# A gated MLP's down projection as seven products of quarter blocks, with weight sums made by DMAs in DRAM

## The chip, the cores and the metric

The kernel runs on one core of a Trainium2 chip. The metric is the device time of one execution in microseconds (us); lower is better. "The profile" is one execution recorded by the hardware profiler; its times count from the first instruction of that execution.

## What is computed

One layer of an encoder trunk on 512 tokens of width 1024: a token mixing stage (attention heads beside a gated recurrent group), a cross-attention into 256 memory tokens, and a gated MLP. The last stage is the one that matters here; the rest is named only so that the stages of the profile can be told apart.

```python
def conv_ffn(h, w_up, conv_w, conv_b, w_down):
    u = h @ w_up                       # 512 x 1024  @  1024 x 5632
    ...                                # depthwise convolution over 3 positions
    gate, val = jnp.split(acc, 2, axis=-1)
    return (jax.nn.silu(gate) * val) @ w_down     # 512 x 2816  @  2816 x 1024

x = x + rmsnorm(conv_ffn(h, ...), post_ffn_g)
```

## The kernel before

**Precision.** Every product is made from numbers split into a high part and a low part of the type fp32r. `mm3` (L149) issues three matmuls for one product: high by high (L150), high by low (L151), low by high (L152). A split (`split`, L103) is a ScalarE cast of the source (L104) and a subtraction on VectorE (L105).

**Weights.** All weights lie in DRAM as units of 128 x 1024 floats, in the order in which they are used. `load_w` (L115) issues the load of the next unit on SP's queue (L117) into one of two "raw" buffers; `issue` (L121) casts and subtracts it into one of four "wh" and four "wl" buffers. For the units 7 to 41 the low part is made another way: a negated copy of the high part (L129 on ScalarE or L131 on POOL), to which a DMA from POOL's queue adds the weights (L132). `unit` (L143) hands out the next unit, and `issue_ahead` keeps three units ahead of it.

**Big buffers.** Activations live in 16 buffers of 8 KB per partition, all called "big" (L94). A tile takes one when it is first written and gives it back after its last use. PSUM has eight banks: two each of the names b, s, c and o.

**The MLP.** For each of 22 chunks of 128 channels, `proj_fm` (L252) makes a gate and a value block from one unit each (24 matmuls), and `conv` (L899) evacuates it: ScalarE scales and adds the bias (L902), VectorE adds the two neighbours (L903, L905), ScalarE applies silu to the gate (L908), VectorE multiplies value and gate (L913) into the tiles `acts`, four chunks to a tile.

**Down projection (L932 to L966).** Eight PSUM banks hold the whole result, four row blocks of 128 tokens by two column halves. For each of the 22 chunks the activations of 512 tokens are split, a unit of weights (128 x 1024) is taken, and 8 x 3 matmuls are issued. The last four chunks are gone through row block by row block, so that the norm and the residual of one block (`residual_part`, L206: square on ScalarE L209, a small chain on POOL L178 and L181, gain on VectorE L211; `residual_add`, L214, L216) and its store (L966) run while TensorE works on the next.

**Order.** The source is written in the order of the data flow, with a `weave` of generators in the earlier stages. The order on each engine is made when the program is built, from which instruction is ready; `tc.issue_after(...)` holds an instruction behind another one on its engine (used around L403 to L425 for the first loads). Each engine then runs its own list strictly in order. POOL's list holds the row scales of all norms (L168, L169, L178, L181), the DMAs of the gains (L163) and the accumulating DMAs (L132). Near the start, L168 makes the row scales of x, from which TensorE spreads the row factors (L405) that the first evacuated projections are multiplied with.

Of the kernel before, what the change touches and what calls it, by code (L numbers as in the profile page):

```python
# [18 lines left out]
P = 128  # L19
# [55 lines left out]
def layer(tc, io, out):  # L75
# [8 lines left out]
    b8 = pool("b8", bufs=16)  # L84
    t4 = pool("t4", bufs=2)
    t2 = pool("t2", bufs=4)

    def small():
# [23 lines left out]
    pending, last_pow, last_mm = deque(), [None], [None]  # L112
    issued, taken, last_load = [0], [0], [None]

    def load_w():  # L115
        raw = rawp.tile([P, 1024], F32, name="raw", tag="raw")
        last_load[0] = nc.sync.dma_start(raw, io["w"][issued[0]]).ins  # L117
        issued[0] += 1
        return raw

    def issue():  # L121
        i = issued[0]
        raw = load_w()
        wh = wp.tile([P, 1024], F32R, name="wh", tag="wh")
        wl = wp.tile([P, 1024], F32R, name="wl", tag="wl")
        if i in NEG_SCALAR or i in NEG_POOL:
            nc.scalar.copy(wh, raw)  # L127
            if i in NEG_SCALAR:
                nc.scalar.mul(wl, wh.bitcast(F32), -1.0)  # L129
            else:  # L130
                nc.gpsimd.tensor_scalar(wl, wh.bitcast(F32), -1.0, 0.0, op0=ALU.mult, op1=ALU.add)  # L131
            nc.gpsimd.dma_start(wl, io["w"][i], accum_op=ALU.add)  # L132
        else:
            split(wh, wl, raw)
        pending.append((wh, wl))
# [13 lines left out]
    def mm3(o, a, b, start, stop):  # L149
        nc.tensor.matmul(o, a[0], b[0], start=start, stop=False)  # L150
        nc.tensor.matmul(o, a[0], b[1], start=False, stop=False)  # L151
        last_mm[0] = nc.tensor.matmul(o, a[1], b[0], start=False, stop=stop).ins  # L152

    def blk(b):
        return slice(b * P, (b + 1) * P)
# [16 lines left out]
    def half(c):  # L172
        return slice(c * 512, c * 512 + 512)
# [137 lines left out]
    def drain(g):  # L311
        for _ in g:
            pass
# [580 lines left out]
    hT = new_act()  # L894
    turns = res_second(ox, range(4), kv["x0"], between(x, g_post, g_pre, hT))

    acts, gates = [], {}

    def conv(c, i, u):  # L899
        g = c * NF + i  # L900
        a = tmp2()
        nc.scalar.activation(a, u, ACT.Identity, scale=cw[:, g, 1:2], bias=cw[:, g, 3:4])  # L902
        nc.vector.scalar_tensor_tensor(out=a[:, 1:], in0=u[:, :T - 1], scalar=cw[:, g, 0:1], in1=a[:, 1:],  # L903
                                       op0=ALU.mult, op1=ALU.add)
        nc.vector.scalar_tensor_tensor(out=a[:, :T - 1], in0=u[:, 1:], scalar=cw[:, g, 2:3], in1=a[:, :T - 1],  # L905
                                       op0=ALU.mult, op1=ALU.add)
        if c == 0:
            nc.scalar.activation(a, a, ACT.Silu)  # L908
            gates[i] = a
        else:  # L910
            if i % 4 == 0:
                acts.append(big([P, 4, T]))
            nc.vector.tensor_mul(acts[-1][:, i % 4, :], gates.pop(i), a)  # L913

    up_tags = "bsco"
    first = [(c, i) for i in range(2) for c in range(2)]
# [16 lines left out]
    y = [[bank(y_tags[c][b]) for c in range(2)] for b in range(NB)]  # L933
    parts = {}

    def down(b, c, kc, w):
        hi, lo = parts[kc // 4]
        mm3(y[b][c], (hi[:, kc % 4, blk(b)], lo[:, kc % 4, blk(b)]), (w[0][:, 0, half(c)], w[1][:, 0, half(c)]),
            kc == 0, kc == NF - 1)

    last = NF - 4
    ws = {}
    for kc in range(NF):
        if kc % 4 == 0:
            parts[kc // 4] = (big([P, 4, T], F32R), big([P, 4, T], F32R))
        split(parts[kc // 4][0][:, kc % 4, :], parts[kc // 4][1][:, kc % 4, :], acts[kc // 4][:, kc % 4, :])
        w = unit(1)
        if kc >= last:
            ws[kc] = w
            continue  # L950
        for b in range(NB):
            for c in range(2):
                down(b, c, kc, w)
    for b in range(NB):
        ss, done = small(), []
        for c in range(2):
            for kc in range(last, NF):
                down(b, c, kc, ws[kc])
            done.append(residual_part(ss, y[b][c], g_post, c, half(c), c == 1, "ta" if c else "th"))
        if b == NB - 1:  # L960
            yg, cols = done.pop()
            for q in range(2):
                done.append((yg[:, q * 256:q * 256 + 256], slice(cols.start + q * 256, cols.start + q * 256 + 256)))
        for i, part in enumerate(done):
            residual_add(ss, part, x[b])
            (nc.sync, nc.scalar)[i % 2].dma_start(out[blk(b), part[1]], x[b][:, part[1]])  # L966
    assert taken[0] == N_UNITS
    ctx.close()


def pack_weights(w_in, w_xkv, w_out, w_xq, w_xo, w_up, w_down):
# [24 lines left out]
    for c in range(8):  # L996
        fm(w_xkv, c * P)
    tm(w_xkv, 1024)
    tm(w_out, 0, MIX_ORDER)
    tm(w_out, 512, MIX_ORDER)  # L1000
    tm(w_xkv, 1536)
    for c in range(8):
        fm(w_xq, c * P)
    tm(w_xo, 0)
    tm(w_xo, 512)
    for i in range(NF):
        fm(w_up, i * P)
        fm(w_up, FF + i * P)
    for kc in range(NF):
        units.append(w_down[kc * P:(kc + 1) * P])  # L1010
    assert len(units) == N_UNITS
    return np.stack(units)


def shape_constants():
# [42 lines left out]
```

## Time and profile before

| | us |
|---|---|
| time, median of 3 runs (839.5 to 841.27) | 839.54 |
| the profiled execution, its own time | 839.84 |
| span of that execution, first to last instruction | 838.1 |
| TensorE busy | 826.9 |
| VectorE busy | 488.0 |
| ScalarE busy | 430.8 |
| POOL busy | 91.8 |

PE is TensorE's matmul side, PEld its weight loads, DVE VectorE, ACT ScalarE, POOL GpSimd, SP the engine that only issues DMAs; a q behind a name is its sequencer. "L105" is line 105 of the kernel. A group's row reads: line, engine, operation, output<-inputs by the program's names, shapes, count | busy us, mean ns of one | idle time of the engine just before, and what ended it. A row of the timeline reads: start, duration, engine, line, operation, and in brackets the idle time before it and its releaser. A row of the stages reads: stretch, its length, then busy time (and instructions) of PE, PEld, DVE, ACT and POOL, then the granted TensorE clock, the busy share of the 16 DMA engines, and GB/s. The digits of the DMA row on the page are tenths in 40 equal slices of the span. A queue's row reads: packets, MB, share of 16 engines' span.

### The profile page before, as it was taken

Reading aid. Unit: us, or ns where it says so; the run is one execution under the profiler, and the core shown is the slowest. Engines: PE = TensorE matmul, PEld = TensorE weight load, DVE = VectorE, ACT = ScalarE, POOL = GpSimd, SP = SyncE. Lnnn points to the kernel's source line nnn. Section 1 sums busy time; section 2 is a strip of 40 time slices with the busy share of each in tenths; the row PEclk is TensorE's granted clock in tenths of the full one; section 3 lists DMA queues with packets and bytes.
Section 4 is the critical chain, followed back from the end, with each engine's and each line's share of the span. In section 5 each row is a group of like instructions: output and inputs, shape, how many; then the busy total and the mean of one; then the engine's idle time right before and its main releaser. Section 6 shows DMA issues by size and latency. Waiting matters only on the chain.

```text
span 838.1 us, 11074 instructions
## 1 busy us (share of the span) xinstructions
PE 826.9 (99%) x4304; PEld 700.8 (84%) x4304; DVE 488.0 (58%) x759; ACT 430.8 (51%) x743; POOL 91.8 (11%) x148
## 2 busy tenths in 40 slices
PE   9999999999999999999999999999999999999996
PEld 7888888889898888888888998888888888888885
DVE  5347577389886866854535765555555557722224
ACT  6676656379888864644534553333333335522221
POOL 0111201145123102200001300000000000000001
PEclk9999999999999999999999999999999999999999
DMA  8696654558677551342311332222222233222212
GB/s 317 191 280 142 158 114 99 129 127 192 139 169 156 127 186 40 126 151 76 101 50 51 122 107 99 101 101 100 99 84 94 101 101 101 100 91 90 97 50 101
DMA packets 29860, 101.81 MB, mean 121 GB/s; under 512 B 3952, under 2 KB 4464, under 8 KB 29808
## 3 DMA queue, kind: packets, MB, share of 16 engines
q1 hardware_dynamic: 22752, 77.38, 26.9%
q0 software_dynamic: 5760, 20.97, 13.9%
q10 hardware_dynamic: 1296, 2.76, 0.9%
q8 instruction: 34, 0.56, 0.3%
q14 instruction: 18, 0.15, 0.1%
HBM read 99.00 MB, written 2.10 MB: 121 GB/s over the span
## 4 chain that ended last, share of the span: by engine, by line
PE 95%; DVE 2%; DMA 1%; ACT 1%; issue 0%; SPq 0%; POOL 0%; POOLq 0%; DVEq 0%
PE ps_b L150 10%; PE ps_b L152 10%; PE ps_b L151 10%; PE ps_s L152 6%; PE ps_s L151 6%; PE ps_s L150 6%; PE ps_o L150 6%; PE ps_o L152 6%; PE ps_o L151 6%; PE ps_c L150 4%; PE ps_c L152 4%; PE ps_c L151 4%; PE ps_c L517 3%; PE ps_o L762 2%; PE ps_s L740 2%; PE ps_o L750 2%
## 5 line engine op out<-in xcount | busy, mean ns | idle before, releaser
L105 DVE TENSOR_TENSOR wl<-raw,wh 128x1024 fp32r<-128x1024 f32 x93 | 113.8, 1224 | 199.6 <-ACT wh L104 199.4
L104 ACT CAST wh<-raw 128x1024 fp32r<-128x1024 f32 x93 | 98.0, 1053 | 205.2 <-PE ps_o L152 71.4
L150 PE MATMUL ps_b<-big,wh 128*128 128x512 f32 (+1 forms) x320 | 118.2, 370 | 0.8 <-DVE big L105 0.8
L152 PE MATMUL ps_b<-big,wl 128*128 128x512 f32 (+1 forms) x320 | 116.6, 364 | 0.0
L151 PE MATMUL ps_b<-big,wh 128*128 128x512 f32 (+1 forms) x320 | 116.5, 364 | 0.0
L150 PEld LDWEIGHTS ps_b<-big,wh 128*128 128x128 f32 x320 | 60.3, 189 | 9.7 <-DVE big L105 0.9
L152 PEld LDWEIGHTS ps_b<-big,wl 128*128 128x128 f32 x320 | 60.3, 189 | 9.3
L151 PEld LDWEIGHTS ps_b<-big,wh 128*128 128x128 f32 x320 | 60.4, 189 | 9.1
L178 POOL TENSOR_SCALAR small<-small 128x1 f32<-128x1 f32 x40 | 13.9, 348 | 439.2 <-ACT tmp L209 420.2
L543 DVE TENSOR_TENSOR big<-big 128x512 f32<-128x512 f32 x64 | 48.4, 761 | 15.1 <-PE ps_c L517 8.8
L150 PE MATMUL ps_s<-wh,big 128*128 128x512 f32 (+1 forms) x140 | 53.7, 383 | 0.4 <-DVE big L105 0.4
L152 PE MATMUL ps_s<-wh,big 128*128 128x512 f32 (+1 forms) x140 | 53.1, 379 | 0.0
L151 PE MATMUL ps_s<-wl,big 128*128 128x512 f32 (+1 forms) x140 | 53.0, 379 | 0.0
L127 ACT CAST wh<-raw 128x1024 fp32r<-128x1024 f32 x35 | 36.8, 1050 | 23.7 <-PE ps_b L151 13.1
L150 PE MATMUL ps_o<-wh,big 128*128 128x512 f32 (+1 forms) x124 | 47.9, 386 | 0.0
L151 PE MATMUL ps_o<-wl,big 128*128 128x512 f32 (+1 forms) x124 | 46.8, 377 | 0.0
L152 PE MATMUL ps_o<-wh,big 128*128 128x512 f32 (+1 forms) x124 | 46.7, 377 | 0.0
L105 DVE TENSOR_TENSOR big<-ps_o,big 128x512 fp32r<-128x512 f32 x54 | 37.1, 688 | 13.4 <-ACT big L104 13.2
L132 POOL DMA_DIRECT2D wl<-in_w_dram x35 | 30.8, 881 | 119.5 <-ACT wl L129 104.5
L104 ACT CAST big<-ps_o 128x512 fp32r<-128x512 f32 x54 | 31.7, 586 | 19.4 <-PE ps_o L865 7.5
L150 PE MATMUL ps_b<-wh,big 128*128 128x512 f32 x92 | 36.9, 401 | 0.0
L151 PE MATMUL ps_b<-wl,big 128*128 128x512 f32 x92 | 36.0, 392 | 0.0
(245 smaller groups left out, 1935.7 us busy)
## 6 DMA issues: line engine op xcount, KB each, us to landing
raw<-in_w_dram SPq DMA_DIRECT2D x131, 512.0 KB, 3.2
wl<-in_w_dram POOLq DMA_DIRECT2D x35, 512.0 KB, 5.5
big<-in_x_dram SPq DMA_DIRECT2D x8, 512.0 KB, 6.4
big<-in_xt_dram SPq DMA_DIRECT2D x3, 512.0 KB, 8.2
big<-in_mem_dram ACTq DMA_DIRECT2D x2, 512.0 KB, 11.9
out_dram<-big SPq DMA_DIRECT2D x4, 256.0 KB, 2.0
out_dram<-big ACTq DMA_DIRECT2D x3, 256.0 KB, 2.0
big<-in_xt_dram SPq DMA_DIRECT2D x2, 256.0 KB, 3.4
```

The costliest lines, as they stand in the source:

```text
L104: nc.scalar.copy(hi, src)
L105: (eng or nc.vector).tensor_sub(lo, src, hi.bitcast(F32))
L127: nc.scalar.copy(wh, raw)
L132: nc.gpsimd.dma_start(wl, io["w"][i], accum_op=ALU.add)
L150: nc.tensor.matmul(o, a[0], b[0], start=start, stop=False)
L151: nc.tensor.matmul(o, a[0], b[1], start=False, stop=False)
L152: last_mm[0] = nc.tensor.matmul(o, a[1], b[0], start=False, stop=stop).ins
L517: nc.tensor.matmul(o[:, b, :], kc[:, blk(b)], pat(qk, b * P, [[2 * m, P // (2 * m)], [T + m, 2], [1, m]]), start=True, stop=True)
L543: nc.vector.tensor_tensor(out=c, in0=c, in1=pat(tt, toff + off, [[2, npair], [gap, 2], [0, m]]), op=ALU.mult)
L740: nc.tensor.matmul(s, qT[h // 4][:, h % 4, blk(qb)], kT[:, 2 * (h // 4) + c, :], start=c == 0, stop=c == 1)
L750: nc.tensor.transpose(o[:, c, :], e[:, 0, blk(c)], ident)
L762: nc.tensor.matmul(o, vv[:, c, h // 4].rearrange("p a d -> p (a d)"), pt[:, j, c, :], start=c + j == 0, stop=c == 3 and j == 1)
```

## The change

The down projection is cut into quarters. The 512 tokens are halved (0 to 255, 256 to 511), the 22 chunks are split into 11 even and 11 odd ones, the 1024 columns are halved. With A for the activations (second index: even or odd chunks) and W for the weights, the four quarters of the result need eight products of quarters if computed directly; the change makes seven (the Winograd form of Strassen's scheme), each of 256 tokens by 11 chunks by 512 columns, and combines them by additions.

- **Weights.** `pack_down` stores the four quarters w11, w12, w21, w22 as 128 x 5632 each. Four sums are needed as well: t1 = w11 + w12, t3 = w22 + w12, t2 = t1 + w22, t4 = t2 + w21 (the signs are put in the combinations). `new_sums(u)` makes slice u of the four: for each a tile in DRAM, a DMA from POOL's queue that copies one operand into it, and a second one that adds the other. Six slices make 48 DMAs; the call stands in the up projection's loop after the chunks 2, 5, 8, 11, 14 and 17. Slices are 1024 columns wide, the last 512.
- **Units.** The 22 units of the down projection become 42: seven products by six slices. Units 0 to 109 are as before. A unit of a product is loaded from the quarter or from the sum in DRAM.
- **Activations.** `conv` writes even and odd chunks to separate tiles; after each eight chunks (and at the end) `group_sides` makes three differences on VectorE: S = A21 - A22, A11 - S, and A21 - A11 in place of A21. The left sides of the seven products are split group by group (three groups of 4, 4 and 3 chunk pairs), three groups ahead; in the group of index 1, products 1 to 6, the low part is made by a negated copy on POOL and an accumulating DMA.
- **Products.** Each product uses two PSUM banks (row blocks 0 and 1 of its half). What is combined is copied or added on ScalarE and VectorE when a product ends. Rows 256 to 511 are finished after the sixth product, rows 0 to 255 after the seventh, whose last four chunk pairs are gone through block by block.

```diff
-N_UNITS = 132
+N_WHOLE, N_UNITS = 110, 152
+NP = NF // 2
+GROUPS = ((0, 4), (4, 8), (8, NP))
+PRODUCTS = (("w11", "b"), ("t2", "s"), ("t1", "c"), ("w22", "o"), ("t3", "s"), ("t4", "c"), ("w21", "b"))
+SUMS = (("t1", "w11", "w12"), ("t3", "w22", "w12"), ("t2", "t1", "w22"), ("t4", "t2", "w21"))
+LAY_AHEAD = 3
+NEG_GROUP = frozenset((p, 1) for p in range(1, 7))
...
+            p, u = divmod(i - N_WHOLE, 6)
+            cols = width(u)
+            raw = raw[:, :cols.stop - cols.start]
+            nc.sync.dma_start(raw, weight_block(PRODUCTS[p][0], cols))
...
+    def new_sums(u):
+        n = width(u).stop - width(u).start
+        for out_name, first_name, second_name in SUMS:
+            t = dram.tile([P, n], F32, name="sum_%s_%d" % (out_name, u), tag="sum_%s_%d" % (out_name, u))
+            nc.gpsimd.dma_start(t, weight_block(first_name, width(u)))
+            nc.gpsimd.dma_start(t, weight_block(second_name, width(u)), accum_op=ALU.add)
+            sums.setdefault(out_name, []).append(t)
+
+    def group_sides(g):
+        n = GROUPS[g][1] - GROUPS[g][0]
+        even, odd = acts[g]
+        t = big([P, 2, 4, 256])
+        sides.append(t)
+        nc.vector.tensor_sub(t[:, 0, :n], even[:, :n, half_t[1]], odd[:, :n, half_t[1]])
+        nc.vector.tensor_sub(t[:, 1, :n], even[:, :n, half_t[0]], t[:, 0, :n])
+        nc.vector.tensor_sub(even[:, :n, half_t[1]], even[:, :n, half_t[1]], even[:, :n, half_t[0]])
...
+            if i % 8 == 7 or i == NF - 1:
+                group_sides(i // 8)
...
+        if i % 3 == 2 and i // 3 < 6:
+            new_sums(i // 3)
...
+    def left_side(p, g):
...
+        if p == 3:
+            nc.vector.tensor_sub(sides[g][:, 1, :n], odd[:, :n, half_t[0]], sides[g][:, 1, :n])
+        src = (even[:, :n, half_t[0]], sides[g][:, 1, :n], sides[g][:, 0, :n], sides[g][:, 1, :n],
+               even[:, :n, half_t[1]], odd[:, :n, half_t[1]], odd[:, :n, half_t[0]])[p]
+        t = big([P, 2, 4, 256], F32R)
+        hi, lo = t[:, 0, :n], t[:, 1, :n]
+        if (p, g) in NEG_GROUP:
+            nc.scalar.copy(hi, src)
+            nc.gpsimd.tensor_scalar(lo, hi.bitcast(F32), -1.0, 0.0, op0=ALU.mult, op1=ALU.add)
+            nc.gpsimd.dma_start(lo, src, accum_op=ALU.add)
+        else:
+            split(hi, lo, src)
...
+    for p, (_, tag) in enumerate(PRODUCTS):
+        y = [bank(tag) for _ in range(2)]
+        for j in range(NP if p < 6 else last):
+            if j % 4 == 0:
+                lay_ahead(3 * p + j // 4)
+            if j % 2 == 0:
+                w = take()
+            for b in range(2):
+                products(y, p, j, w, b)
+        if p == 0:
+            y1, u = tmp4([P, 2, 512]), tmp4([P, 2, 512])
+            for b in range(2):
+                nc.scalar.copy(y1[:, b], y[b])
+        elif p == 1:
+            for b in range(2):
+                nc.vector.tensor_sub(u[:, b], y[b], y1[:, b])
...
+        for i, cols in enumerate(pieces):
+            nc.vector.tensor_add(c11[:, cols], y[b][:, cols], y1[:, b, cols])
+            parts[b].append(residual_part(rows[b], c11[:, cols], g_post, 1 + i, cols, i == b, "th"))
+        finish(b, rows[b], parts[b])
```

More of the change, by code (lines that the diff above doesn't have):

```diff
@@ L113, in layer, with weight_block, width @@
     issued, taken, last_load = [0], [0], [None]
+    sums = {}
+    def weight_block(name, cols):
+        if name in sums:
+            return sums[name][cols.start // 1024][:, :cols.stop - cols.start]
+        return io["wd"][("w11", "w12", "w21", "w22").index(name)][:, cols]
+    def width(u):
+        return slice(u * 1024, min(u * 1024 + 1024, NP * 512))
     def load_w():
         raw = rawp.tile([P, 1024], F32, name="raw", tag="raw")
-        last_load[0] = nc.sync.dma_start(raw, io["w"][issued[0]]).ins
+        i = issued[0]
+        if i < N_WHOLE:
+            last_load[0] = nc.sync.dma_start(raw, io["w"][i]).ins
+        else:
[3 more added lines that the diff above has]
+            nc.sync.dma_start(raw, weight_block(PRODUCTS[p][0], cols))
         issued[0] += 1
@@ L910, in conv @@
         else:
[L911 to L913 removed]
+            if i % 8 == 0:
+                acts.append([big([P, 4, T]) for _ in range(2)])
+            nc.vector.tensor_mul(acts[-1][i % 2][:, i // 2 % 4, :], gates.pop(i), a)
+            if i % 8 == 7 or i == NF - 1:
+                group_sides(i // 8)
     up_tags = "bsco"
@@ L942, in layer @@
[L942 to L963, printed above, removed]
+    def left_side(p, g):
+        n = GROUPS[g][1] - GROUPS[g][0]
+        even, odd = acts[g]
+        if p == 3:
[8 more added lines that the diff above has]
+            nc.gpsimd.dma_start(lo, src, accum_op=ALU.add)
+        else:
+            split(hi, lo, src)
+        return hi, lo
@@ new lines, in layer, with lay_ahead, products, take @@
+    order = [(p, g) for p in range(7) for g in range(3)]
+    laid = {}
+    def lay_ahead(i):
+        while len(laid) < min(len(order), i + LAY_AHEAD):
+            laid[order[len(laid)]] = left_side(*order[len(laid)])
+    def products(y, p, j, w, b):
+        hi, lo = laid[p, j // 4]
+        ac, wc = (slice(None), j % 4, blk(b)), half(j % 2)
+        mm3(y[b], (hi[ac], lo[ac]), (w[0][:, wc], w[1][:, wc]), j == 0, j == NP - 1)
+    def take():
+        taken[0] += 1
+        issue_ahead()
+        return pending.popleft()
@@ new lines, in layer @@
+    lay_ahead(20)
+    ws = {}
+    for j in range(last, NP):
+        ws[j] = take() if j % 2 == 0 else ws.get(j - 1, w)
+    for b in range(2):
+        c11 = tmp2(tag="tq")
+        pieces = [slice(0, 256), slice(256, 512)] if b else [slice(0, 512)]
+        for j in range(last, NP):
+            products(y, 6, j, ws[j], b)
+        for i, cols in enumerate(pieces):
+            nc.vector.tensor_add(c11[:, cols], y[b][:, cols], y1[:, b, cols])
+            parts[b].append(residual_part(rows[b], c11[:, cols], g_post, 1 + i, cols, i == b, "th"))
+        finish(b, rows[b], parts[b])
@@ L1008, in pack_weights, with pack_down @@
         fm(w_up, FF + i * P)
-    for kc in range(NF):
-        units.append(w_down[kc * P:(kc + 1) * P])
-    assert len(units) == N_UNITS
+    assert len(units) == N_WHOLE
     return np.stack(units)
+def pack_down(w_down):
+    w = w_down.reshape(NP, 2, P, 2, 512).transpose(1, 3, 2, 0, 4)
+    return w.reshape(4, P, NP * 512)
 def shape_constants():
```

41 lines of the change are left out of this document (31 added, 10 removed).

## The prediction

> **What bounds the kernel now.** I read the page from the top: engines, slices, DMA queues, chain, then the DMA issues.
>
> ```profile
> PE 826.9 (99%) x4304; PEld 700.8 (84%) x4304; DVE 488.0 (58%) x759; ACT 430.8 (51%) x743; POOL 91.8 (11%) x148
> ...
> DMA  8696654558677551342311332222222233222212
> ...
> q1 hardware_dynamic: 22752, 77.38, 26.9%
> q0 software_dynamic: 5760, 20.97, 13.9%
> ...
> PE 95%; DVE 2%; DMA 1%; ACT 1%; issue 0%; SPq 0%; POOL 0%; POOLq 0%; DVEq 0%
> ...
> raw<-in_w_dram SPq DMA_DIRECT2D x131, 512.0 KB, 3.2
> wl<-in_w_dram POOLq DMA_DIRECT2D x35, 512.0 KB, 5.5
> ```
>
> TensorE is busy for 826.9 of 838.1 us and holds 95% of the chain. A matmul taken away shortens the kernel, provided that nothing new makes TensorE wait. The DMA slices matter for this change: the first ones are nearly full, the late ones run at two or three tenths. Next come the stages (last three columns: clock, DMA share, GB/s) and the two ends of the down projection on the TensorE timeline.
>
> ```profile
> 0.00:60.00 60.00, 57.95 (x256) 47.32 (x257) 26.90 (x50) 39.76 (x58) 7.03 (x14) 1.00 0.84 262
> 60.00:200.00 140.00, 139.42 (x842) 120.40 (x841) 97.31 (x176) 89.53 (x153) 29.99 (x38) 1.00 0.59 136
> 200.00:230.00 30.00, 28.14 (x214) 26.06 (x212) 25.99 (x62) 25.00 (x51) 10.55 (x14) 1.00 0.68 159
> 230.00:340.00 110.00, 109.77 (x659) 94.65 (x660) 78.88 (x150) 81.70 (x179) 24.22 (x39) 1.00 0.51 130
> 480.00:700.00 220.00, 220.00 (x1027) 184.58 (x1027) 122.92 (x145) 85.51 (x105) 0.00 (x0) 1.00 0.30 100
> 720.00:800.00 80.00, 80.00 (x354) 66.25 (x353) 22.20 (x24) 17.35 (x18) 0.00 (x0) 1.00 0.30 99
> ```
> ```profile
> 711.38 0.39 PE L152 MATMUL ps_o<-big,wl 128*128 128x512 f32 x1
> 711.61 0.39 PE L150 MATMUL ps_b<-wh,big 128*128 128x512 f32 x1
> ...
> 831.28 0.39 PE L152 MATMUL ps_o<-wh,big 128*128 128x512 f32 x1
> ```
>
> The last up matmul starts at 711.38, the first down matmul at 711.61: no gap. All 528 down matmuls (22 chunks, 4 row blocks, 2 halves, 3 terms) start between 711.61 and 831.28, so one costs 119.67/527 = 0.227 us.
>
> **Step 1, fewer matmuls.** Seven products of 11 chunks, 2 row blocks and 3 terms are 462. 66 x 0.227 = **15.0 us saved**, all on the path.
>
> **Step 2, the weight loop.** Before, a unit of weights feeds 24 matmuls (5.44 us); now a full unit feeds 12 (2.72 us), and 22 units become 42 (35 full, 7 half). Each passes load, ScalarE cast and VectorE subtraction in one of two raw buffers. The rows, for the down stage and for 600 to 838 us:
>
> ```profile
> DMA to landing us min/median/max: 3.1/3.2/3.8
> ```
> ```profile
> L105 DVE TENSOR_TENSOR wl<-raw,wh 128x1024 fp32r<-128x1024 f32 x41 | 50.2, 1225 | 117.1 <-ACT wh L104 117.1
> L104 ACT CAST wh<-raw 128x1024 fp32r<-128x1024 f32 x41 | 43.2, 1054 | 118.4 <-PE ps_o L152 70.8 <-PE ps_c L151 18.6 <-PE ps_b L151 18.6
> ...
> L105 DVE TENSOR_TENSOR big<-big 128x512 fp32r<-128x512 f32 x22 | 13.8, 688 | 0.0
> L104 ACT CAST big<-big 128x512 fp32r<-128x512 f32 x22 | 12.0, 619 | 1.2 <-DVE big L105 1.2
> ```
>
> Now the cast waits for TensorE to free a buffer, so the loop has room. One round of one raw buffer is 3.2 + 1.05 + 1.23 + some 0.06 between them = 5.54 us and serves every second unit. TensorE consumes two full units in 5.44 us and a product in 66 x 0.227 = 15.0 us. A product has six units, so one buffer always carries three full ones: 3 x 5.54 = 16.6 us. The loop falls behind by 1.65 us per product even without a collision.
>
> There will be collisions. VectorE in the down stage: 35 x 1.23 + 7 x 0.69 = 48 us for weights; 15 of the 21 left sides, 17 us at 1.23 us per 1024 elements; three differences for the fourth product, 3; some 15 additions on PSUM at 0.69, 10; the residual, 12. That is 90 us in a stage of 105. ScalarE comes to 70. A unit that waits 0.5 us in all for the two engines (between nothing and the 1.0 of half an operation on each) adds 3 x 0.5 = 1.5 us per product. The slip over seven products is 7 x (1.65 + 1.5) = 22 us. The slack is three units ahead, 8.2 us, less cast and subtraction, 2.3: 5.9. **16 us of TensorE waiting** remain (6 at no collision, 27 at 1.0 us). What queues behind a late subtraction on VectorE is the evacuation of a finished product and the next left side.
>
> **Step 3, the seam.** The up projection ends with a convolution, and the new differences of the last group follow it. The rows on either side:
>
> ```profile
> 702.33 2.17 ACT L104 CAST big<-big 128x512 fp32r<-128x512 f32 x4
> ...
> 711.81 0.78 ACT L902 ACTIVATE tmp<-ps_o,cw 128x512 f32<-128x512 f32 x1
> ```
> ```profile
> 712.97 0.75 DVE L903 SCALAR_TENSOR_TENSOR tmp<-ps_o,cw,tmp 128x511 f32<-128x511 f32 x1
> 713.63 1.22 DVE L105 TENSOR_TENSOR wl<-raw,wh 128x1024 fp32r<-128x1024 f32 x1
> 714.76 0.75 DVE L905 SCALAR_TENSOR_TENSOR tmp<-ps_o,cw,tmp 128x511 f32<-128x511 f32 x1
> 715.42 0.69 DVE L105 TENSOR_TENSOR big<-big 128x512 fp32r<-128x512 f32 x1
> 716.02 0.69 DVE L913 TENSOR_TENSOR big<-tmp,tmp 128x512 f32<-128x512 f32 x1
> ```
>
> Before, the first four chunks were split at 702, nine us ahead. Now all sixteen "big" buffers are taken there (x 2, hT 4, gains 1, products of the gate 6, differences 3), so the first left side waits for a buffer of hT, which the up projection reads to its end. Its cast can run after the 902 at about 712.6. Its subtraction stands behind the 903, 905 and 913, then three differences of 768 elements, at 0.96 each by the two sizes above: 712.6 + 2.0 + 2.8 + 1.2 = 718.6. TensorE has about four matmuls that need only the cast (0.9 us). The hole is 718.6 - 711.6 - 0.9 = 6; I take **5.5 us** (2 if the subtraction is laid ahead of the differences, 7 if weights come between). The Trainium skill, "TensorE: Matmul & The Clock Gate", section "What's actually happening", says that TensorE falls to half rate after an idle window of about 3.4 us and stays there for as long again; by that the hole would cost some 1.7 us more (an estimate from that page). No gap of this trace is long enough to show it.
>
> The nine differences made during the up projection lie beside TensorE, with VectorE at 122.92 of 220 us: nothing. The six left sides that go over POOL and an accumulating DMA have 15 us of lead against 1.05 + 1.05 + 5.5: nothing. The tail gains an addition of 256 columns and the next small chain, **0.6 us**.
>
> **Step 4, the sums in DRAM.** 24 copies and 24 accumulating DMAs of 512 KB go to POOL's queue. Their price by queue: q1 moved 77.38 MB in 26.9% of 838.1 us, 1.53 us of all 16 engines per 512 KB; q0 moved 20.97 MB in 13.9%, 116.5 us, and without the five gain loads at 1.53 that leaves 109/35 = 3.1 us per accumulating DMA. 24 x 1.53 + 24 x 3.1 = 111 us of transfers. (An accumulation into DRAM does not occur here; nearest are the load's 1.53 below and the 5.5 us landing above.) Beside the up projection, with 70% of the DMA free for 220 us, they would cost nothing. **But where do they run?** The diff writes them into the up loop, yet nothing holds them there: they read only inputs and need no on-chip buffer. The trace shows what becomes of such an instruction. L582 is written behind the turn of the memory rows (L194, ps_s):
>
> ```profile
> L582 DVE TENSOR_SCALAR qkg<-qkg x1: 187/187/187, 28.6 to 28.6; 128x64 f32<-128x64 f32 x1
> ```
> ```profile
> L194 PE MATMUL ps_s<-ident,big x8: 271/272/273, 128.1 to 129.3; 128*128 128x128 f32 x8
> ```
> ```profile
> 0.87 0.11 POOL L324 MEMSET nhalf<- 128x16 f32 x1
> 22.79 0.20 POOL L168 TENSOR_SCALAR rx<-rx 128x4 f32<-128x4 f32 x1 [21.81 <-ACT tmp L394]
> ...
> 37.12 1.07 POOL L132 DMA_DIRECT2D wl<-in_w_dram  x1 [8.68 <-ACT wl L129]
> ```
>
> L582 ran 100 us before its neighbour in the source, as soon as its operand had landed. By the same rule the copies float to the front of POOL's stream, into the idle 21.81 us before L168, and the additions follow as copies land. There the DMA engines are 84% busy. Behind the sums on POOL wait the row scales (L168, on which the first projections wait) and the accumulations of weights (L132), which TensorE needs three units later; SP's loads share the engines.
>
> The cost is what the idle DMA time does not take in. Free are 0.16 x 60 = 10 us to 60, 0.41 x 140 = 57 more to 200, 0.32 x 30 = 10 to 230, 0.49 x 110 = 54 to 340. Had all 111 us to be through before what is now 60 us, the kernel would lose 101; before 200, 44; before 230, 34; before 340, nothing. I take **40 us** (0 to 101), nearest to the middle: the DMA queue is shared, so the sums neither come first nor last. The Trainium skill, "DMA: Bandwidth & Descriptors", section "Anatomy of one DMA", prices a DMA from POOL at 2.0 us plus bytes/436e3. By that an accumulating one lands after 3.2 us; the row says 5.5, so the trace disagrees. With 1.2 us of transfer each (an estimate from that page) the sums would be 58 us, and the term nothing if they were through by 200.
>
> **The sum.** The profiled execution took 839.84 us, 838.1 of them span, close to the median of 839.54. 839.8 - 15.0 + 16 + 5.5 + 0.6 + 40 = **887 us**.
>
> **Rivals.** (1) The sums stay harmless, by their place or because early DMA gaps take them in; the weight loop still binds: 847, between 837 and 858. For it: 70% free DMA from 480 on. Against: L582. (2) The other side: the sums are harmless and the loop keeps up. This is decided by the round of a raw buffer: with 5.9 us of slack over seven products it may slip 0.84 per product, so a round of at most 5.27 us, a landing of 2.9 instead of 3.2. Then 839.8 - 15 + 5.5 + 0.6 = 831, up to 837. Against: the minimum landing is 3.1. (3) The sums keep the source's place behind POOL's last work before the up loop, and chain: six dependent DMAs per slice and six slices. At 5.5 us that is 198 us, in time; at 8, 288 us, and the second product, due some 15 us after the first, waits about 13: 860.
>
> **Chances.** Forecast 0.58 (857 to 940), rival 1 0.22, rival 2 0.13, rival 3 0.07. The range 834 to 935 leaves out most of rival 2 and the top of the forecast. A measurement tells 0.2% (1.7 us) from no change: faster 0.13 (rival 2), within 0.04 (the low end of rival 1), slower 0.83.
>
> **What would show it.** Step 1: 462 down matmuls at 0.227. Step 2: ScalarE's casts wait on the raw DMA instead of TensorE, and TensorE waits on wh and wl in the down stage. Step 3: a hole of TensorE of 5 to 6 us after the last up matmul. Step 4: sum DMAs on POOL before 60 us, L168 and L132 later, TensorE idle before 230 us. If the sums appear only after 480 us, the 40 us fall and rivals 1 to 3 remain; if casts still wait on TensorE, step 2 falls.

## The result, and the profile after

The changed kernel takes **923.72 us** (median of 4 runs, 923.15 to 925.53); the kernel before, on the same chip, 840.15 (4 runs, 839.5 to 841.27). The ratio is 1.0997, with a 95% interval of 1.0976 to 1.1018. The forecast was 887.

First the page of the changed kernel, from the top: engines, slices, queues, chain, DMA issues with the median time to landing.

```profile
PE 840.2 (91%) x4238; PEld 701.4 (76%) x4238; DVE 533.1 (58%) x800; ACT 457.5 (50%) x766; POOL 143.6 (16%) x209
...
PE   7683977999999999999999999999999996987884
...
PEclk9887898999999999999999999999999998999998
DMA  9999998746595763234222143232222332569453
...
q0 software_dynamic: 13216, 47.19, 24.2%
...
PE 67%; DMA 16%; DVE 6%; issue 5%; POOL 3%; ACT 3%; SPq 0%; POOLq 0%; DVEq 0%; ACTq 0%
...
sum_t<-in_wd_dram POOLq DMA_DIRECT2D x30, 512.0 KB, 9.9
...
sum_t<-sum_t POOLq DMA_DIRECT2D x10, 512.0 KB, 7.5
```

TensorE issues 66 matmuls fewer and is busy for longer: some of them ran at a lower clock, as the PEclk row shows (tenths of full speed, 40 slices). Its idle time lies in the first seven slices and the last seven; between them the row is all nines. Before, it was nines but for the last slice:

```profile
PE   9999999999999999999999999999999999999996
```

DMA, 1% of the chain before, is 16% now. The DMA row shows why in front: six full slices.

The stages of the changed kernel (length, then busy time and count of PE, PEld, DVE, ACT, POOL, then clock, DMA share, GB/s). A DMA share a little above 1 means that the engines were full. The last three stretches are the seam, the matmuls behind it, and the rest of the down projection.

```profile
0.00:60.00 60.00, 42.99 (x145) 32.61 (x146) 18.23 (x33) 21.26 (x34) 17.27 (x29) 0.86 0.95 295
60.00:140.00 80.00, 54.34 (x268) 44.41 (x267) 26.17 (x45) 37.13 (x59) 21.26 (x29) 0.85 1.03 285
...
480.00:700.00 220.00, 220.00 (x1079) 186.12 (x1078) 127.10 (x154) 88.78 (x130) 11.11 (x25) 1.00 0.28 94
770.14:778.86 8.72, 1.59 (x7) 0.68 (x5) 7.30 (x9) 5.28 (x6) 0.00 (x0) 0.77 0.12 32
778.86:785.30 6.44, 6.44 (x16) 5.04 (x17) 5.54 (x5) 1.05 (x1) 0.00 (x0) 0.52 0.00 0
785.30:911.30 126.00, 110.25 (x444) 84.95 (x442) 69.22 (x74) 56.48 (x70) 18.54 (x21) 0.96 0.60 171
```

From 480 to 700, where the source writes the sums, the DMA share is 0.28: they are not there. They are in front. POOL's timeline of the changed kernel has the first sum, the row scales of x, the first accumulation of weights and the last sum:

```profile
1.31 1.82 POOL L930 DMA_DIRECT2D sum_t<-in_wd_dram  x3 [0.34 <-issue]
...
47.54 0.20 POOL L194 TENSOR_SCALAR rx<-rx 128x4 f32<-128x4 f32 x1 [3.58 <-ACT tmp L420]
...
66.23 0.93 POOL L158 DMA_DIRECT2D wl<-in_w_dram  x1
...
164.10 0.84 POOL L931 DMA_DIRECT2D sum_t<-in_wd_dram  x1 [4.04 <-DMA sum_t<-sum_t]
```

The row scales are made at 47.54 (before: 22.79), the first accumulation is issued at 66.23 (before: 37.12), and the last sum at 164.10. What TensorE waited for up to 200 us says what this cost (in total, times, longest):

```profile
PE ps_s L177 <- DMA wl<-in_w_dram: 17.2, 2, 11.0
PE ps_c L597 <- DVE tmp L593: 11.0, 1, 11.0
PE ps_s L407 <- ACT wh L383: 9.8, 3, 5.1
PE ps_b L176 <- ACT wh L111: 5.8, 1, 5.8
```

The first row is the accumulations of weights, which POOL issues. L593 on VectorE waited for row scales of a later norm from POOL. So 28.2 of these 43.8 us are waits for what stands behind the sums on POOL's list. The other 15.6 us wait for ScalarE's casts of the first weights; ScalarE itself waited there for loads (13.9 us for weights, 7.6 for x).

The seam and the end of the down projection on TensorE's timeline, then the same seam on VectorE and ScalarE, in the changed kernel:

```profile
770.14 0.39 PE L178 MATMUL ps_o<-big,wl 128*128 128x512 f32 x1
773.05 0.50 PE L176 MATMUL ps_b<-wh,big 128*128 128x512 f32 x1 [2.52 <-ACT big L111]
...
778.86 1.22 PE L178 MATMUL ps_b<-wh,big 128*128 128x512 f32 x2 [4.61 <-DVE big L112]
...
780.30 0.63 PE L177 MATMUL ps_b<-wl,big 128*128 128x512 f32 x1
780.73 0.63 PE L178 MATMUL ps_b<-wh,big 128*128 128x512 f32 x1
...
911.03 0.39 PE L178 MATMUL ps_b<-wh,big 128*128 128x512 f32 x1
```
```profile
771.42 1.23 DVE L112 TENSOR_TENSOR wl<-raw,wh 128x1024 fp32r<-128x1024 f32 x1 [2.76 <-ACT wh L111]
...
774.85 0.96 DVE L939 TENSOR_TENSOR big<-big 128x768 f32<-128x768 f32 x1
...
776.72 0.95 DVE L941 TENSOR_TENSOR big<-big 128x768 f32<-128x768 f32 x1
777.59 4.36 DVE L112 TENSOR_TENSOR big<-big 128x1024 fp32r<-128x1024 f32 x4
```
```profile
771.97 3.66 ACT L111 CAST big<-big 128x1024 fp32r<-128x1024 f32 x4
```

The hole is the one that was forecast, instruction by instruction: cast behind the last activation, subtraction behind the three differences. A unit of weights came between (771.42), and the convolution's first addition starts only behind it, at 772.56. The rows after 778.86 show something more: the matmuls start 0.43 us apart instead of 0.227, in a stretch with a granted clock of 0.52.

In the weight loop ScalarE's casts wait for the loads now, as the waits of the changed kernel say (in total, times, longest):

```profile
ACT wh L111 <- DMA raw<-sum_t: 28.9, 16, 4.3
...
ACT wh L111 <- DMA raw<-in_wd_dram: 16.9, 7, 5.6
```

At the end VectorE takes block 0's last two residual additions (L242) ahead of block 1's last PSUM additions (L1069), though TensorE was through at 911.4:

```profile
912.61 1.42 DVE L242 SCALAR_TENSOR_TENSOR big<-tmp,small,big 128x512 f32<-128x512 f32 x2 [0.79 <-POOL small L207]
913.94 0.75 DVE L1069 TENSOR_TENSOR tmp<-ps_b,tmp 128x256 f32<-128x256 f32 x2
```

These rows give the account of the 84.2 us between the spans (922.3 - 838.1):

| | forecast | measured | from |
|---|---|---|---|
| ahead of the last up matmul (step 4) | +40 | +58.8 | 770.14 - 711.38 |
| 66 matmuls (step 1) | -15.0 | -15.2 | shown below by a version without waits |
| seam (step 3) | +5.5 | +10.4 | 2.5 + 4.6 idle, 15 matmuls of 0.2 us too much, 0.3 around them |
| weight loop (step 2) | +16 | +25.8 | the rest of the stage: 140.9 (911.03 - 770.14) - 119.9 + 15.2 - 10.4 |
| end | +0.6 | +4.4 | (922.3 - 911.03) - (838.1 - 831.28) |

### The profile page after: what moved, and what is told of

The parts are those of the page before. It is cut to its first block, busy times and chain, and to the rows that moved or that the text cites. A ratio compares the mean times of both kernels' runs of the same rounds, so it can differ in the third digit from the quotient of the medians.

```text
span 922.3 us, 11153 instructions
## 1 busy us (share of the span) xinstructions
PE 840.2 (91%) x4238; PEld 701.4 (76%) x4238; DVE 533.1 (58%) x800; ACT 457.5 (50%) x766; POOL 143.6 (16%) x209
## 4 chain that ended last, share of the span: by engine, by line
PE 67%; DMA 16%; DVE 6%; issue 5%; POOL 3%; ACT 3%; SPq 0%; POOLq 0%; DVEq 0%; ACTq 0%
PE ps_b L178 8%; PE ps_b L177 7%; PE ps_b L176 7%; DMA sum_t<-in_wd_dram 5%; PE ps_s L176 4%; PE ps_s L178 4%; PE ps_s L177 4%; PE ps_o L176 4%; DMA raw<-sum_t 4%; PE ps_o L177 4%; PE ps_o L178 4%; PE ps_c L176 3%; PE ps_c L177 3%; PE ps_c L178 3%; DMA big<-in_x_dram 3%
## 5 line engine op out<-in xcount | busy, mean ns | idle before, releaser
L112 DVE TENSOR_TENSOR wl<-raw,wh 128x1024 fp32r<-128x1024 f32 (+1 forms) x113 | 134.3, 1190 | 177.5 <-ACT wh L111 177.2
L111 ACT CAST wh<-raw 128x1024 fp32r<-128x1024 f32 (+1 forms) x113 | 115.7, 1024 | 197.2 <-PE ps_b L177 53.3
L176 PE MATMUL ps_b<-big,wh 128*128 128x512 f32 (+1 forms) x320 | 120.2, 376 | 6.5 <-ACT wh L111 5.8
L177 PE MATMUL ps_b<-big,wh 128*128 128x512 f32 (+1 forms) x320 | 117.9, 369 | 0.0
L178 PEld LDWEIGHTS ps_b<-big,wl 128*128 128x128 f32 x320 | 61.1, 191 | 10.4 <-DVE wl L112 0.8
L569 DVE TENSOR_TENSOR big<-big 128x512 f32<-128x512 f32 x64 | 48.4, 761 | 32.9 <-PE ps_c L543 25.8
L176 PE MATMUL ps_s<-wh,big 128*128 128x512 f32 (+1 forms) x140 | 55.2, 398 | 2.0 <-ACT wh L111 1.6
L178 PE MATMUL ps_s<-wh,big 128*128 128x512 f32 (+1 forms) x140 | 55.1, 394 | 0.0
L993 POOL TENSOR_SCALAR big<-big 128x1024 fp32r<-128x1024 f32 x6 | 6.3, 1054 | 290.6 <-ACT big L992 290.6
L153 ACT CAST wh<-raw 128x1024 fp32r<-128x1024 f32 x35 | 36.8, 1050 | 27.5 <-PE ps_o L178 11.4
L177 PEld LDWEIGHTS ps_s<-wl,big 128*128 128x128 f32 x140 | 27.7, 198 | 24.0 <-DMA wl<-in_w_dram 18.1
L176 PE MATMUL ps_b<-wh,big 128*128 128x512 f32 x92 | 38.7, 424 | 5.9 <-ACT wh L111 3.4
L178 PE MATMUL ps_b<-wh,big 128*128 128x512 f32 x92 | 38.0, 415 | 4.6 <-DVE big L112 4.6
L176 PE MATMUL ps_o<-wh,big 128*128 128x512 f32 (+1 forms) x102 | 39.5, 392 | 2.9 <-ACT wh L111 2.9
L204 POOL TENSOR_SCALAR small<-small 128x1 f32<-128x1 f32 x41 | 17.9, 436 | 152.1 <-ACT tmp L235 133.0
```

Source lines behind the costliest of these rows:

```text
L111: nc.scalar.copy(hi, src)
L112: (eng or nc.vector).tensor_sub(lo, src, hi.bitcast(F32))
L204: nc.gpsimd.tensor_scalar(ss[:, i + 4:i + 5], ss[:, i:i + 1], 1.0 / D, ss[:, i + 3:i + 4] if i else EPS, op0=ALU.mult, op1=ALU.add)
L569: nc.vector.tensor_tensor(out=c, in0=c, in1=pat(tt, toff + off, [[2, npair], [gap, 2], [0, m]]), op=ALU.mult)
L993: nc.gpsimd.tensor_scalar(lo, hi.bitcast(F32), -1.0, 0.0, op0=ALU.mult, op1=ALU.add)
```

## The experiments

**Theory:** the loss is four separate things: sums in front of POOL's list, two raw buffers for units that feed half as many matmuls, a left side that is ready too late at the seam, and VectorE's order at the end. **Rivals:** the sums cost much wherever they run; the stage's waits come from contention (accumulating DMAs beside loads) and not from the buffers; and, for the front, POOL's order and not the shared DMA time is what costs.

| run | median us (runs) | ratio to before, 95% interval |
|---|---|---|
| e1_held | 865.77 (4) | 1.0291 [1.0273, 1.0308] |
| e2_sums_alone | 900.50 (4) | 1.0712 [1.0678, 1.0746] |
| e3_held_raw3 | 845.84 (4) | 1.0052 [1.0033, 1.0071] |
| e4_held_seam | 856.71 (4) | 1.0174 [1.0148, 1.0200] |
| e5_all | 834.14 (5) | 0.9912 [0.9896, 0.9928] |
| e6_no_neg | 860.42 (4) | 1.0229 [1.0206, 1.0251] |
| e7_end | 864.11 (4) | 1.0277 [1.0260, 1.0295] |
| e8_copies_alone | 882.43 (4) | 1.0484 [1.0463, 1.0505] |
| e9_narrow_sums | 859.21 (4) | 1.0215 [1.0196, 1.0234] |
| e10_behind_rows | 905.65 (4) | 1.0771 [1.0751, 1.0791] |
| e11_all_no_neg | 829.35 (4) | 0.9866 [0.9851, 0.9880] |

The kernel before took 841.16 beside e1 to e4, 840.80 beside e5 to e8, and 840.19 beside e9 to e11. e5 to e8 ran on another chip than the other runs.

**e1_held: the sums held at the source's place.** `last_pow[0]` is POOL's last row scale written so far.

```diff
         if i % 3 == 2 and i // 3 < 6:
-            new_sums(i // 3)
+            with tc.issue_after(last_pow[0]):
+                new_sums(i // 3)
```

> The changed kernel with the 48 sum DMAs held behind POOL's last row scale of the cross-attention (about 475 us). Theory (the place of the sums made the 58.8 us by which the first down matmul is late): the down stage starts at 711.6 us again as before, the sums are all done before it, and the time is 923.7 - 58.8 = 865 us. Rival A (48 DMAs cost TensorE time wherever they run, by taking DMA time from the weight loads): the start falls back by less than half, time above 890 us. Rival B (they chain too slowly at the later place): the start is back, but TensorE waits on raw tiles loaded from the sums in the second product, time 870 to 885 us.

865.77: 58 us less than the changed kernel. The window of the sums in this run:

```profile
470.00:600.00 130.00, 130.00 (x673) 111.75 (x672) 79.04 (x94) 51.81 (x68) 34.74 (x51) 1.00 0.97 274
```

POOL issues the first sum at 476.5 and the last at 604.8 now. They fill the DMA engines (0.97), and TensorE is busy for 130.00 of 130 us: there they cost nothing. The rival that they cost much anywhere falls. The down stage, from the last up matmul to the last down matmul, is about as long as in the changed kernel (139.9 us here, 140.9 there).

**e2_sums_alone: the kernel before with the sums added**, as the change writes them, and read by nobody.

```diff
             drain(proj_fm(hT, T, up_tags[(2 * i + c) % 4], lambda u: conv(c, i, u)))
+        if i % 3 == 2 and i // 3 < 6:
+            new_sums(i // 3)
```

> The kernel before with only the 48 sum DMAs added, in the same place of the source and not held; nothing reads the sums, the down projection is the old one. Theory (the sums in front of POOL's list are the whole loss ahead of the down stage): 840.2 + 58.8 = 899 us, with TensorE idle before 230 us. Rival (the rest of the change, for example its other order of units or of POOL's work, has a share in the early loss): below 885 us.

59.3 us slower than before (900.5 - 841.16), against 58.8 lost in front in the changed kernel. The front loss belongs to the sums alone; in e2's trace the last up matmul starts at 770.99, before at 711.38.

**e3_held_raw3: held, with three raw buffers**; room for the third is taken from the temporaries.

```diff
-    rawp = pool("rawp", bufs=2)
+    rawp = pool("rawp", bufs=3)
-TMP_BUFS = {'ta': 4, 'th': 4, 'tq': 3}
+TMP_BUFS = {'ta': 3, 'th': 3, 'tq': 3}
```

> Sums held, and three raw buffers instead of two (one tmp buffer of two kinds fewer to make room, which can cost something in the earlier stages; the down stage is read by itself). Theory (the round of a raw buffer, landing + cast + subtraction, makes the 25 us of waits in the down stage): casts wait on the raw DMA no more, the waits fall under 8 us, time about 865 - 18 = 847 us. Rival (VectorE and ScalarE, whose own work is in the way, make the waits): the waits stay above 18 us, time above 858 us.

845.84, which is 19.9 less than e1. The waits of TensorE in the weight loop of this run (the seam's 4.6 and 2.5 us stand ahead of them):

```profile
PE ps_o L176 <- ACT wh L111: 1.3, 1, 1.3
PE ps_o L177 <- DVE wl L112: 0.9, 1, 0.9
PE ps_b L177 <- DVE wl L112: 0.3, 1, 0.3
```

2.5 us are left in the loop, of 15.7 in the changed kernel. One more buffer is enough, with the same loads and the same engines: what bound was the round of a raw buffer.

**e4_held_seam: held, with the first three left sides laid earlier**: two before the last up chunk, the third right behind the loop and ahead of the last group's differences. (`left_side` is moved ahead of the loop; it picks the source of product 0 by itself, since the last differences don't exist yet when it is called.)

```diff
+        if i == NF - 2:
+            for g in range(2):
+                laid[0, g] = left_side(0, g)
+    laid[0, 2] = left_side(0, 2)
+    group_sides(2)
...
-            if i % 8 == 7 or i == NF - 1:
+            if i % 8 == 7:
                 group_sides(i // 8)
```

> Sums held, and the first two left sides of the first product are split one chunk before the end of the up projection, ahead of the last group's differences. Theory (the hole at the seam, 2.7 + 4.8 us, and 3 us of half-rate matmuls behind it, come from the order of the last differences and from the full big buffers): hole under 1 us, no half-rate matmuls there, time 865 - 9 = 856 us. Rival (the weight loop uses the hole to get ahead, so that it is only moved): the waits later in the stage grow by as much, time 862 to 866 us.

856.71, 9.1 less than e1. The rows at the seam:

```profile
711.23 0.39 PE L178 MATMUL ps_o<-big,wl 128*128 128x512 f32 x1
711.46 0.39 PE L176 MATMUL ps_b<-wh,big 128*128 128x512 f32 x1
```

No hole is left.

**e7_end: held, with block 0's last residual additions held behind block 1's last PSUM addition.** `add` is that addition.

```diff
-        finish(b, rows[b], parts[b])
+        if b:
+            with tc.issue_after(add):
+                finish(0, rows[0], parts[0])
+            finish(1, rows[1], parts[1])
```

> Sums held, and block 0's last residual held behind block 1's last PSUM addition on VectorE; nothing else. Theory (2.5 of the 4.4 us by which the end is longer are block 0's residual standing ahead of block 1's addition): the end from the last matmul to the last instruction falls from 11.0 to about 8.7 us, time 863.5 us. Rival (the longer chain itself, addition, square, POOL, makes it): no change, 865.8 us.

864.11 against e1's 865.77; the intervals overlap. In the traces the last down matmul starts 10.2 us before the end of the span here (862.2 - 852.00), 11.4 in e1 (863.7 - 852.27) and 6.8 in the kernel before. So the order on VectorE is about 1 us of the 4.4; the rest of the end was not taken apart.

**e6_no_neg: held, with no accumulating DMA in the down stage**; the six left sides that went over POOL are split on ScalarE and VectorE.

```diff
-NEG_GROUP = frozenset((p, 1) for p in range(1, 7))
+NEG_GROUP = frozenset()
```

> Sums held, and the low parts of all left sides by VectorE's subtraction, none by POOL and an accumulating DMA. Theory A (the weight loop is bound by a round of landing + cast + subtraction, and the six accumulating DMAs lengthen landings from 3.2 us to 5 and more): landings in the down stage fall to 3.2 to 3.5 us, the waits shrink by some 5 us, time about 861 us. Theory B (VectorE's own load is in the way): six more subtractions of 1.22 us, 7 us in all, lengthen the waits, time 868 to 873 us.

860.42, some 5 less than e1, though VectorE has six more operations. The rival of contention has a share, then, but not the main one: without those DMAs e6's casts still waited 33.2 us for loads (41 in e1), and TensorE 12.4 us in the loop (14.3 in e1). The trace is of e6's slowest run, 862.64. The full loads from the quarters landed after 4.1 us by the median of the stage, where they took 4.5 in e1.

**e5_all: e1, e3, e4 and e7 together**, with the edits above.

> Sums held, third raw buffer, seam undone, and the last residual of row block 0 held behind the last PSUM addition of block 1. Theory (the four losses are separate and add up): 865.8 - 19.9 (third buffer) - 9.1 (seam) - 2 (end) = 835 us, faster than the kernel before by about 0.7%. Rival (the losses hide one another: without the seam's hole the weight loop has less lead, so the third buffer gives back less): 840 to 848 us.

834.14: 0.88% faster than the kernel before (0.72 to 1.04%). The sum of the single gains, 865.8 - 19.9 - 9.1 - 1.7 = 835.1, is what came out: the repairs do not overlap.

**e11_all_no_neg: e5 with e6's edit.**

> The version with all four repairs (sums held, three raw buffers, left sides ahead of the seam, the order at the end), and the left sides of the middle group split on ScalarE and VectorE, so that no accumulating DMA runs in the down stage. If the lengthened landings still cost something with three raw buffers: 829 to 832 us. If three buffers have covered them already: 834, or up to 836, since VectorE takes six more subtractions of 1.23 us. Taken: 833, the waits of the stage being some 3 us.

829.35, ratio 0.9866: the fastest version of this study, 1.3% faster than before. I had taken 833; the accumulating DMAs still cost some 4 us with three raw buffers (3.9 by the ratios of e5 and e11; the down stage took 108.5 us in e5). Page and window of this run:

```profile
PE 812.8 (98%) x4238; PEld 688.6 (83%) x4238; DVE 537.0 (65%) x806; ACT 455.8 (55%) x766; POOL 130.8 (16%) x197
...
DMA  9696754666678543342212199999952233366652
```
```profile
713.47:818.60 105.13, 105.10 (x464) 86.74 (x462) 83.89 (x90) 60.10 (x74) 7.07 (x11) 1.00 0.58 180
```

The DMA row has the sums as six full slices in the middle, where the kernel before had twos and threes. The down stage, from the last up matmul (713.47) to the last down matmul (818.19), takes 104.7 us, and TensorE is busy in all of it at full clock. Before, it took 119.9: step 1's saving is 15.2 us and lies open only now.

**Three runs on what the sums cost in front.** All three are the kernel before with sums that nobody reads. e8 replaces the 24 additions by plain copies of the same size; e9 keeps the additions but makes every DMA 64 columns wide; e10 keeps everything and holds the sums behind the row scales of x.

```diff
-            nc.gpsimd.dma_start(t, weight_block(second_name, width(u)), accum_op=ALU.add)
+            nc.gpsimd.dma_start(t, weight_block(second_name, width(u)))
```

> The kernel before with 48 plain copies in place of 24 copies and 24 accumulating DMAs, in front of POOL's list as in the run with the sums alone; the tiles in DRAM hold a copy of the second operand instead of a sum, and nothing reads them. Theory (the early loss is transfer time: 44 full-size DMAs, half of them at 3.1 us, the others at 1.5): with all at 1.5 us the transfers fall from about 102 to 67 us and the loss by at least as much, from 59 to about 20 us, time 860 us. Rival (POOL's waits for landings make it, whatever moves): the number of waits is the same, the loss stays above 45 us, time above 885 us.

```diff
-            nc.gpsimd.dma_start(t, weight_block(first_name, width(u)))
-            nc.gpsimd.dma_start(t, weight_block(second_name, width(u)), accum_op=ALU.add)
+            nc.gpsimd.dma_start(t[:, :64], weight_block(first_name, width(u))[:, :64])
+            nc.gpsimd.dma_start(t[:, :64], weight_block(second_name, width(u))[:, :64], accum_op=ALU.add)
```

> The kernel before with the 48 sum DMAs added in front as in the changed kernel, in the same order and with the same dependences, but each only 64 columns wide (32 KB in place of 512 KB; nobody reads the sums). POOL still has to issue all of them and to wait for each copy before the addition that follows it; the transfers shrink to a sixteenth (102 us of all 16 engines to some 7). Theory A, shared DMA time: with 33 us and more of free DMA time ahead of 140 us, the loss goes: 841 to 846 us. Theory B, POOL's order: a wait of some 2 us at each of 24 additions still stands ahead of the row scales and the accumulations of weights: 850 to 870 us. Taken: A, 844.

```diff
     r = rstd_of(rx[:, :NB], NB, D, rx[:, NB:])
+    rows_done = last_pow[0]
...
-            new_sums(i // 3)
+            with tc.issue_after(rows_done):
+                new_sums(i // 3)
```

> The kernel before with the 48 full sum DMAs added (nobody reads them), but held behind the row scales of x on POOL's list (some 24 us), so that only the weights' accumulations and the later row scales stand behind them. Theory A, shared DMA time: the same 102 us of transfers then fall into the stretch from 24 us on; what is lost ahead of 60 us shrinks, but the loss is only shifted: 895 to 903 us, as the 900.5 without the hold. Theory B, the late row scales of x are the price of the first 24 us: 870 to 880. Taken: A with some relief, since the loads of x and of the first weights get the engines to themselves: 892.

All three came out above the value that I had taken. The queue rows of e2, e8 and e9 (packets, MB, share of 16 engines' span) give the time of the transfers, less the 116.5 us that this queue took before:

```profile
q0 software_dynamic: 11200, 44.05, 22.6%
```
```profile
q0 software_dynamic: 10944, 44.05, 20.0%
```
```profile
q0 software_dynamic: 9984, 22.55, 15.2%
```

| | transfers added, us of 16 engines | loss, us |
|---|---|---|
| e9 | 0.152 x 859.1 - 116.5 = 14.1 | 859.21 - 840.19 = 19.0 |
| e8 | 0.200 x 877.8 - 116.5 = 59.1 | 882.43 - 840.80 = 41.6 |
| e2 | 0.226 x 898.3 - 116.5 = 86.5 | 900.5 - 841.16 = 59.3 |

The loss grows by 0.50 us per us of transfers from e9 to e8, and by 0.65 from e8 to e2 (transfers from one profiled run each, losses from medians). So making the transfers full-sized adds the larger part of the loss (40 of 59 us), and some of what is added still vanishes in free DMA time. The 19 us of e9 need almost no transfers: the row scales of x stand behind narrow sums and come at 44.34 instead of 22.79, and TensorE, which spreads the row factors made from them (L418), waits for that in one piece.

```profile
44.34 0.20 POOL L181 TENSOR_SCALAR rx<-rx 128x4 f32<-128x4 f32 x1
```
```profile
46.91 2.08 PE L418 MATMUL ps_c<-tmp,ones 128*128 128x128 f32 x8 [14.77 <-DVE tmp L411]
```

The row scales are 21.6 us late, and this one wait is 14.8 of the 19 us lost. But e10, with the row scales of x in time, loses 65.5, more than e2. From its POOL timeline, and TensorE's waits up to 200 us:

```profile
23.39 0.20 POOL L181 TENSOR_SCALAR rx<-rx 128x4 f32<-128x4 f32 x1 [22.41 <-ACT tmp L407]
...
189.13 0.81 POOL L918 DMA_DIRECT2D sum_t<-in_wd_dram  x1 [2.79 <-DMA sum_t<-sum_t]
```
```profile
PE ps_c L585 <- DVE tmp L581: 33.3, 2, 17.9
PE ps_s L164 <- DMA wl<-in_w_dram: 23.3, 2, 22.8
```

The last sum is then issued at 189, and the weights' accumulations and the row scales of a later norm (for which L581 waits) stand between the sums. The casts of the first weights are nearly in time here (0.3 us of waits), so the relief that I had hoped for came, and POOL's list took more than it gave. Narrow sums ahead of the row scales of x suffice to lose 19 us; with full transfers, bringing these row scales forward gives nothing back. Neither POOL's order nor shared DMA time is the cause alone: POOL waits for each copy to land before it issues the addition, so slow transfers make its list slow. These runs do not split the 59 us into two shares that add up.

## Why the prediction was right, and where it was wrong

The sign was right, and so was the case: the forecast, with the sums floating to the front. The time is 36.7 us above the 887, and it lies in the range that was given because step 4 had been left open from 0 to 101.

**Step 1 (-15.0) was right:** -15.2 in e11.

**Step 2 (+16) had the right mechanism.** Casts wait on raw loads, and a third buffer removes it. The 16 us of waiting are what the trace has: of the loop's 126.00 us TensorE is busy for 110.25, so 15.7 are idle. That the two agree so closely is luck, since the working took 1.5 us of collisions per product between bounds of 0 and 3. Missing was what a wait drags behind it: three stretches of about eight matmuls start 0.43 us apart behind waits (24 x 0.2 = 4.8 us), and the matmuls right beside the 14 waits come late by the remaining 5. That makes 25.8. Inside it two sizes were off: the full loads from the quarters landed after 4.8 us by the median of the stage (from the sums 3.3), where the working had 3.2; and the six left sides over POOL, put at nothing, cost some 5 us (e6) or 4 (e11).

**Step 3 (+5.5) had the right chain and the wrong sum.** Idle were 7.1 us, the upper end of the 2 to 7 that were given, for the reason given there: weights came between. And 15 matmuls at 0.43 instead of 0.227 us came on top: 3.0. The Trainium skill, "TensorE: Matmul & The Clock Gate", section "What's actually happening", gives the half rate after an idle window of some 3.4 us and an equal time to come back. The rule is borne out in kind behind the 4.61 us here, and the 1.7 us that the prediction set beside it, without adding them, was the right sign; the trace has 6.4 us at half rate, and half of that is lost.

**The end (+0.6) was mis-sized:** 4.4. The prediction counted an addition and a chain for block 1 and left out that VectorE takes block 0's last residual additions first. Of the 3.8 us too much e7 explains about 1; the cause of the rest stays open.

**Step 4 (+40) is the term that failed most:** 58.8. The step was "I take 40, nearest to the middle: the DMA queue is shared, so the sums neither come first nor last". They came first: nothing held them, they were issued from 1.31 us on and the last at 164.10, with the engines at 1.03 from 60 to 140. The prediction's own list had 44 us for "before 200" and 101 for "before 60"; 59 lies between, as the place does. Two errors of size went the other way: the sixth slice is only 512 columns wide, so its eight DMAs are half ones and the sums come to 44 full DMAs and not 48 (102 us by the prediction's prices), and e2's queue shows 86.5. With less transfer than priced, more was lost. The prediction named L168 and L132 as standing behind the sums on POOL, but it priced only the DMA time; 28.2 of TensorE's 43.8 us of waits in front are for what stands there. The price by the Trainium skill, "DMA: Bandwidth & Descriptors", section "Anatomy of one DMA" (2.0 us plus bytes/436e3, an estimate of 3.2 us here) is not what these rows show: 9.9 and 7.5 us to landing in front.

**Rivals.** Rival 1 assumed harmless sums and gave 847; e1 is that case and took 865.8, because steps 2 and 3 and the end were 18 us too cheap. Rival 2, a loop that keeps up, at 831, came about only with the sums held, a third buffer, an earlier left side, the other order at the end and no accumulating DMAs: 829.35. What decided it was the round of a raw buffer, as that rival said, but the round was relieved by a buffer more and not by a faster load. Rival 3 fell with its condition: the sums did not stay in the source's place. Where e1 held them there, POOL issued them all within 128 us, against the 198 to 288 of that rival.

## What to carry to other kernels

Ask of every added instruction what holds it where it is written: one that read only inputs ran first here, and "beside idle engines later" is a plan only with a hold. When a product is halved, halve the time that each operand buffer has for its round, and count buffers again before counting matmuls. Ask what an engine's list holds behind an added DMA that waits for another, and not only what the DMAs move. Price a wait of TensorE above its length: the matmuls behind it can be slow too.

## What the runs showed of the hardware

- TensorE went to half rate behind some short waits. In the changed kernel, behind 2.28 and 0.76 us of idle time at 813 to 815, eight matmuls start 0.43 us apart, and the first of them comes 1.3 us after TensorE is busy again. Waits of 1.82 and 0.71 us at 833, or of 1.98 at 874, were not followed by it, so the length of a wait alone does not decide. The stretch at 813:

```profile
813.34 0.50 PE L176 MATMUL ps_c<-wh,big 128*128 128x512 f32 x1 [2.28 <-ACT wh L111]
814.60 0.50 PE L177 MATMUL ps_c<-wl,big 128*128 128x512 f32 x1 [0.76 <-DVE wl L112]
...
816.34 0.63 PE L177 MATMUL ps_c<-wl,big 128*128 128x512 f32 x1
816.76 0.63 PE L178 MATMUL ps_c<-wh,big 128*128 128x512 f32 x1
```

- A plain copy of 512 KB from DRAM to DRAM took 59.1/44 = 1.34 us of the 16 engines, and an accumulating one (86.5 - 22 x 1.34)/22 = 2.6. Both are estimates, from the queue's time less the 116.5 us of before. They are a little below the 1.53 of a load and the 3.1 of an accumulation into SBUF. Only the landing was longer, 8.7 us in e1 even where the loads of weights alone ran beside.
- A DMA share of 0.97 over 130 us did not slow a stage that TensorE bounds (e1), although the loads of weights landed there after 7.6 us by the median (480 to 600) instead of 3.3 over the whole kernel.
